# A two-layer hybrid encoder step: the output projection and the residual stream from feature-major to token-major, and retention's padded queries made by another engine

## The chip, the cores and the metric

The kernel runs on 1 core of one Trainium2 chip. The metric is the device time of one execution in microseconds, lower is better. The kernel before takes 2413.29 us, the median of 3 runs (2411.71 to 2414.96). All data are 32-bit floats. Every large product is computed in three passes on numbers split into a high and a low part.

## The reference

Two layers run over 1152 tokens: 1024 of a prompt and 128 of eight running streams (nine chunks of 128 tokens). D_MODEL is 1024, the mixer width 2048. Each layer computes the following, and a root-mean-square norm closes the network:

```python
hn = rmsnorm(x, norm_w)
proj = jnp.einsum("btd,dc->btc", hn, w_in).astype(f32)
# four branches (mLSTM, retention, SSD, HGRN2), each a chunkwise recurrence with its own gate
mix = jnp.concatenate([out_m, out_r, out_s, out_h], axis=-1).astype(x.dtype)
y = x + jnp.einsum("btc,cd->btd", mix, w_out)
# after the last layer
return rmsnorm(x, final_norm_w), stacked
```

Retention, per head and chunk, scores queries against keys and adds what the state gives:

```python
s = jnp.einsum("bhlk,bhsk->bhls", q, k) * dec
o = einsum("bhls,bhsv->bhlv", s, v) + decayed * einsum("bhlk,bhkv->bhlv", q, s_prev)
```

## The kernel before

Weights come in slabs of 256 columns. `slab_load` (L348) fetches one, `slab_split` (L362) splits it into `hi` and `lo` (ScalarE copies the high part, VectorE or GpSimd subtracts), and `slab_run` (L378) multiplies. It has two forms. In "fm" (feature-major, L396 to L413) 128 weight columns are stationary and 384 tokens move: 6 output tiles a slab, each 8 x 3 matmuls of 384 columns (L404 to L406). In "tm" (token-major, L414 to L436) 128 tokens are stationary and the slab's 256 columns move: 9 chunk tiles a slab, each 8 x 3 matmuls of 256 columns (L425 to L427). Both load new weights for every matmul.

Ten units (HGRN2 `h`, retention `r`, SSD `s`, mLSTM `m`) share out the input projection. While TensorE projects one unit, the recurrence (`mix`) of the unit before is woven into the same instruction stream by `merge` (L1775), which counts steps of both. Work that is to come some steps later is put off with `later(lag, ...)` and issued by `tick` (L176), which comes twice in each output tile of either form. Nothing is reordered after that: each engine runs its instructions in this written order, and one that waits holds up all behind it.

The output projection (`out_half`, L1916) runs after the units, in two halves of the mixer width, four slabs each. Half 0 is woven with the last HGRN2 recurrence, half 1 runs alone. Before the change all eight slabs are "fm", and x lives feature-major in DRAM (`xd`). For layer 0's half 0 the input is token-major, so `flip` (L1854) transposes each of the 24 tiles on TensorE and ScalarE copies it back. `ev` (L1919) adds the product to x, and in half 1 sums squares over features with ScalarE and VectorE (`sumsq`, L499).

At the end of half 1 `finish` (L1909) runs for each group of 384 tokens. In layer 0 it sums over partitions with a matmul against ones (`colsum`, L507) and makes the next layer's split input (`norm_group`, L513). In layer 1 `final` (L1960) takes the sums, transposes 24 blocks a group back to token-major, scales and stores them.

In retention's `mix` (L1018) `Z` transposes queries and keys of a chunk and copies them from PSUM on ScalarE; `by_head` (L719) then makes the queries padded per head, on GpSimd; `A` (L1042) scores. In mLSTM's `mix` the first `Z` (L950) is also a `by_head` on GpSimd, written after `use_wi(0)` (L797), whose product needs a row loaded from DRAM. In SSD's `conv` (L1171) the first group of a channel tile clears three columns on GpSimd (L1179).

Of the kernel before, what the change touches and what calls it, by code (L numbers as in the profile page):

```python
# [120 lines left out]
class Kernel:  # L121
    def __init__(self, nc, tc, ctx, T):
# [9 lines left out]
        self.p_t = pool("t", 9)  # L132
# [88 lines left out]
    def setup(self):  # L221
# [3 lines left out]
        self.xd = [self.p_dram.tile([KT, 128, NTOK], F32, name=f"xd{i}") for i in range(2)]  # L225
# [273 lines left out]
    def sumsq(self, acc, x, first):  # L499
        if first:  # L500
            self.act(acc, x, AF.Square)
        else:
            sq = self.f()
            self.act(sq, x, AF.Square)
            self.tt(acc, acc, sq, ALU.add)

    def colsum(self, acc):  # L507

        ps = self.ps("tr")[:, :G3]
        self.nc.tensor.matmul(ps, self.ones, acc, start=True, stop=True)  # L510
        return ps

    def norm_group(self, l, g, pre, ss, spread):  # L513

        nc = self.nc
        r = self.f()
        self.act(r, ss, AF.Ln, scale=1.0 / D, bias=self.eps)
        self.act(r, r, AF.Exp, scale=-0.5)
        hi = self.p_big.tile([128, KT, G3], F32R, tag="big", name=self.nm("hnh"))
        lo = self.p_big.tile([128, KT, G3], F32R, tag="big", name=self.nm("hnl"))  # L520

        def part(k):
            nc.vector.scalar_tensor_tensor(out=pre[k], in0=pre[k], scalar=self.vB[:, 8 * l + k:8 * l + k + 1], in1=r,
                                           op0=ALU.mult, op1=ALU.mult)
            self.copy(hi[:, k], pre[k], "a")
            self.tt(lo[:, k], pre[k], hi[:, k].bitcast(F32), ALU.subtract, "v" if k % 2 else "p")

        for k in range(KT):
            if spread:
                self.later(k // spread, lambda k=k: part(k))  # L530
            else:
                part(k)
        self.hn[0][g], self.hn[1][g] = hi, lo
# [197 lines left out]
    def unit_m(self, l, p):  # L731
# [38 lines left out]
        def mix():  # L770
# [175 lines left out]

            load_e(0)
            load_wi(0)
            use_wi(0)
            Z(0)  # L950
# [31 lines left out]
    def unit_r(self, l, p):  # L982
# [35 lines left out]
        def mix():  # L1018
            S = self.p_st.tile([128, 2, 128], F32, tag="st", name=self.nm("rS"))
            nc.gpsimd.memset(S, 0.0)  # L1020
            qkT, Pt, om, mx, stt, U, qz = {}, {}, {}, {}, {}, {}, {}
# [8 lines left out]
            def Z(c):  # L1030
                j, i = divmod(c, 2)
# [3 lines left out]
                t = self.t(256)  # L1035
                self.copy(t, tr[:, 0:256], "a")
                qkT[c] = t
                if c == 8:
                    U["zq"] = [self.zq(t[:, 0:128], slice(64 * h, 64 * h + 64)) for h in range(2)]
# [9 lines left out]
            def B(c):  # L1049
# [16 lines left out]
                if c < 8:  # L1066
# [3 lines left out]
                    for h in range(2):  # L1070
                        hs = slice(64 * h, 64 * h + 64)
                        new = tr[hs, 128 * h:128 * h + 128]
                        if c == 0:
                            self.copy(S[hs, h], new, "v")
                        else:
                            self.tt(S[hs, h], S[hs, h], new, ALU.add)
                    nc.vector.tensor_scalar(out=S, in0=S, scalar1=g_, scalar2=None, op0=ALU.mult)
                    if c == 7:
                        for h in range(2):
                            self.dma(T["o_p_r"][l, 2 * p + h], S[64 * h:64 * h + 64, h])  # L1080
# [42 lines left out]
            qz[0] = self.by_head(qkT[0][:, 0:128])  # L1123
# [898 lines left out]
```

## Time and profile before

| what | value |
|---|---|
| median of 3 runs | 2413.29 us |
| profiled execution | 2415.16 us |
| its span, first to last instruction | 2413.4 us |
| mean granted TensorE clock | 0.988 |
| TensorE matmul busy | 2333.9 us, 97% |
| VectorE, ScalarE, GpSimd busy | 1390.7, 1076.4, 976.2 us |

The span is the time from the first to the last instruction of the core; 1.8 us of the execution lie outside of it. Stretches are given in microseconds from the span's start. A matmul's duration in the trace overlaps with the next one's, since they are pipelined, so a rate is read from the number of matmuls in a stretch and not from their mean duration. PEclk is the granted clock of TensorE: 1.00 is 2.4 GHz, 0.50 is 1.2 GHz.

### The profile page before, as it was taken

The numbers are of one execution on the slowest core, as the hardware profiler recorded it, in microseconds if no ns is written. First come the engines' busy times: TensorE is split into PE (matmuls) and PEld (weight loads), VectorE is DVE, ScalarE is ACT, GpSimd is POOL, SyncE is SP. The second block draws the span as 40 slices with busy tenths as digits, with TensorE's granted clock in tenths as the row PEclk, the third lists the DMA queues.
The fourth block names the chain that finished last, engine by engine and source line by source line (L and its number), as shares of the span: only waits on it lengthen the run. The fifth ranks groups of instructions, "written<-read, shape, count | busy, mean of one in ns | idle before, by whom it ended". The sixth has DMA issues, their size and how long they took to land.

```text
span 2413.4 us, 49607 instructions
## 1 busy us (share of the span) xinstructions
PE 2333.9 (97%) x18992; PEld 2258.8 (94%) x18992; DVE 1390.7 (58%) x3419; ACT 1076.4 (45%) x2780; POOL 976.2 (40%) x1179
## 2 busy tenths in 40 slices
PE   7999999999999998999989999999999999999998
PEld 7999999999999998899988999999899999888998
DVE  4756753773765376544368376537737654666443
ACT  6344563434455345433243445634344653454332
POOL 2443344353334335423135334432633452345353
PEclk9999999999999999999989999999999999999999
DMA  5111233221123222536411212323111333225552
GB/s 151 37 49 45 81 91 77 65 60 52 50 83 95 61 72 74 158 114 213 133 37 37 61 54 80 90 65 77 49 48 55 98 78 81 50 85 167 159 170 82
DMA packets 273736, 204.06 MB, mean 85 GB/s; under 512 B 57908, under 2 KB 264140, under 8 KB 273500
## 3 DMA queue, kind: packets, MB, share of 16 engines
q1 hardware_dynamic: 273180, 200.81, 29.2%
q8 instruction: 150, 2.46, 0.4%
q14 instruction: 86, 0.70, 0.1%
q0 software_dynamic: 320, 0.09, 0.0%
HBM read 148.53 MB, written 52.29 MB: 83 GB/s over the span
## 4 chain that ended last, share of the span: by engine, by line
PE 83%; DVE 8%; ACT 3%; issue 2%; DMA 1%; POOL 1%; SPq 1%; DVEq 0%; ACTq 0%; POOLq 0%
PE w L425 11%; PE w L404 11%; PE w L427 11%; PE w L426 11%; PE w L406 11%; PE w L405 11%; DVE f L212 3%; ACT f L215 2%; PE w L1310 1%; SPq L218 1%; DVE c L212 1%; PE w L1624 1%; PE w L1663 1%; PE w L1061 1%; PE w L833 1%
## 5 line engine op out<-in xcount | busy, mean ns | idle before, releaser
L425 PE MATMUL w<-hi,hnh 128*128 128x256 f32 (+1 forms) x2592 | 775.8, 299 | 0.0
L427 PE MATMUL w<-hi,hnl 128*128 128x256 f32 (+1 forms) x2592 | 731.9, 282 | 1.6 <-DVE hnl L492 1.6
L426 PE MATMUL w<-lo,hnh 128*128 128x256 f32 (+1 forms) x2592 | 731.7, 282 | 0.1
L425 PEld LDWEIGHTS w<-hi,hnh 128*128 128x128 f32 x2592 | 493.0, 190 | 6.1 <-issue 1.1
L426 PEld LDWEIGHTS w<-lo,hnh 128*128 128x128 f32 x2592 | 493.1, 190 | 3.5 <-issue 0.3
L427 PEld LDWEIGHTS w<-hi,hnl 128*128 128x128 f32 x2592 | 492.5, 190 | 2.2 <-DVE hnl L492 2.0
L215 ACT ACTIVATE f<-f 128x384 f32<-128x384 f32 (+1 forms) x475 | 244.1, 516 | 434.8 <-DVE f L212 275.0
L215 ACT ACTIVATE c<-c 128x512 f32<-128x512 f32 (+3 forms) x398 | 211.3, 534 | 292.4 <-DVE c L546 205.4
L212 POOL TENSOR_TENSOR f<-f,f 128x384 f32<-128x384 f32 (+2 forms) x268 | 226.7, 854 | 283.3 <-ACT f L215 210.3
L404 PE MATMUL w<-hnh,hi 128*128 128x384 f32 x960 | 339.3, 353 | 0.0
L212 POOL TENSOR_TENSOR lo<-raw,hi 128x512 fp32r<-128x512 f32 x148 | 195.0, 1318 | 332.3 <-ACT hi L202 279.2
L406 PE MATMUL w<-hnh,lo 128*128 128x384 f32 x960 | 324.6, 338 | 0.0
L405 PE MATMUL w<-hnl,hi 128*128 128x384 f32 x960 | 324.3, 338 | 0.0
L404 PE MATMUL w<-mxh,hi 128*128 128x384 f32 x768 | 268.7, 350 | 0.0
L406 PE MATMUL w<-mxh,lo 128*128 128x384 f32 x768 | 261.1, 340 | 0.0
L405 PE MATMUL w<-mxl,hi 128*128 128x384 f32 x768 | 260.9, 340 | 0.0
L212 POOL TENSOR_TENSOR c<-c,c 128x512 f32<-128x512 f32 (+2 forms) x120 | 128.9, 1083 | 221.2 <-ACT c L215 175.6
L212 DVE TENSOR_TENSOR lo<-raw,hi 128x512 fp32r<-128x512 f32 x140 | 114.4, 817 | 134.4 <-ACT hi L202 134.2
L404 PEld LDWEIGHTS w<-hnh,hi 128*128 128x128 f32 x960 | 181.6, 189 | 3.0 <-issue 1.8
L405 PEld LDWEIGHTS w<-hnl,hi 128*128 128x128 f32 x960 | 181.8, 189 | 0.8
L406 PEld LDWEIGHTS w<-hnh,lo 128*128 128x128 f32 x960 | 181.0, 189 | 0.0
L212 DVE TENSOR_TENSOR c<-c,w 128x384 f32<-128x384 f32 (+1 forms) x124 | 73.3, 595 | 184.8 <-PE w L406 121.6
(304 smaller groups left out, 3979.3 us busy)
## 6 DMA issues: line engine op xcount, KB each, us to landing
raw<-in_w_in SPq DMA_DIRECT2D x224, 128.0 KB
raw<-in_w_in SPq DMA_DIRECT2D x112, 256.0 KB
c<-mixd SPq DMA_DIRECT2D x96, 192.0 KB
raw<-in_w_out SPq DMA_DIRECT2D x64, 256.0 KB
xd<-c SPq DMA_DIRECT2D x66, 192.0 KB
mixd<-c SPq DMA_DIRECT2D x48, 256.0 KB
c<-xd SPq DMA_DIRECT2D x60, 192.0 KB
c<-sscr SPq DMA_DIRECT2D x36, 256.0 KB
```

Source lines behind the costliest of these rows:

```text
L212: (self.nc.vector if e == "v" else self.nc.gpsimd).tensor_tensor(out=out, in0=a, in1=b, op=op)
L215: self.nc.scalar.activation(out=out, in_=in_, func=func, scale=scale, bias=bias, **k)
L218: (e or self.nc.sync).dma_start(out=out, in_=in_)
L404: nc.tensor.matmul(o, hi[:, k, ms], xhi[:, k, :], start=(k == 0), stop=False)
L405: nc.tensor.matmul(o, hi[:, k, ms], xlo[:, k, :], start=False, stop=False)
L406: nc.tensor.matmul(o, lo[:, k, ms], xhi[:, k, :], start=False, stop=(k == KT - 1))
L425: nc.tensor.matmul(o, xhi[:, k, ts], hi[:, k, :w], start=(k == 0), stop=False)
L426: nc.tensor.matmul(o, xhi[:, k, ts], lo[:, k, :w], start=False, stop=False)
L427: nc.tensor.matmul(o, xlo[:, k, ts], hi[:, k, :w], start=False, stop=(k == KT - 1))
L833: nc.tensor.matmul(sc[:, 0:256], k[g][:, cs], qz.pop(c), start=True, stop=True)
L1061: nc.tensor.matmul(po[h], w[:, h], v[j][:, i, h], start=(c in (0, 8)), stop=(c == 0 or (c < 8 and h == 1)))
L1310: nc.tensor.matmul(po[:, 64 * h:64 * h + 64], pt[:, h], x_[:, 64 * h:64 * h + 64], start=True, stop=True)
```

## The change

All eight slabs of the output projection become "tm": the mixed sequence is stationary, w_out moves. `xd` is kept as nine chunks of 128 tokens x 1024 features, x is fetched two chunks by 256 features at a time, and `flip` goes. `ev` adds on VectorE, ScalarE sums squares of each chunk with its accumulator one tick later, and GpSimd multiplies slabs 0 to 2 with the norm's weight, which now lies along the free axis (`wb`, two rows broadcast from DRAM). `finish` runs for each pair of chunks in the last slab of half 1: two small additions, the inverse root, and the scaling of four pieces. In layer 1 the pieces are stored as they are. In layer 0 `enter` transposes each chunk (8 transposes on TensorE) and splits it out of PSUM into the next layer's input. `sumsq`, `colsum`, `norm_group` and `final` go.

In retention VectorE makes the padded queries from PSUM in `Z`, into a tile of the pool "f" beside the keys; the state is one 128-column tile, and each head's query takes its own product with it (two of 128 columns in place of one of 256). In mLSTM `Z(0)` is written ahead of the loads. In `conv` the clearing goes: the taps of the first group start later instead. The pool "t" has 8 tiles in place of 9.

```diff
-        self.p_t = pool("t", 9)
+        self.p_t = pool("t", 8)
...
-        self.xd = [self.p_dram.tile([KT, 128, NTOK], F32, name=f"xd{i}") for i in range(2)]
+        self.xd = [self.p_dram.tile([NCH, 128, D], F32, name=f"xd{i}") for i in range(2)]
...
+    def enter(self, c, y):
+        g, o = divmod(c * 128, G3)
+        if o == 0:
+            self.hn[0][g] = self.p_big.tile([128, KT, G3], F32R, tag="big", name=self.nm("hnh"))
+            self.hn[1][g] = self.p_big.tile([128, KT, G3], F32R, tag="big", name=self.nm("hnl"))
+        for a in range(2):
+            ps = self.ps("tr")
+            for b in range(4):
+                nc.tensor.transpose(ps[:, 128 * b:128 * b + 128], y[2 * a + b // 2][:, 128 * (b % 2):128 * (b % 2) + 128], self.ident)
+            p3 = ps.rearrange("p (k t) -> p k t", k=4)
+            hi, lo = [x[g][:, 4 * a:4 * a + 4, o:o + 128] for x in self.hn]
+            self.copy(hi, p3, "a")
+            self.tt(lo, p3, hi.bitcast(F32), ALU.subtract)
...
+            Z(0)
             load_e(0)
             load_wi(0)
             use_wi(0)
-            Z(0)
...
-                t = self.t(256)
-                self.copy(t, tr[:, 0:256], "a")
+                t = self.f()
+                self.tt(t[:, 0:256].rearrange("p (h t) -> p h t", h=2), tr[:, None, 0:128].to_broadcast([128, 2, 128]),
+                        self.HM[:, :, None].to_broadcast([128, 2, 128]), ALU.mult)
+                self.copy(t[:, 256:384], tr[:, 128:256], "a")
...
-                nc.tensor.matmul(sc, qkT[c][:, 128:256], qz.pop(c), start=True, stop=True)
+                nc.tensor.matmul(sc, qkT[c][:, 256:384], qkT[c][:, 0:256], start=True, stop=True)
...
-                if 0 < c < 8:
-                    nc.tensor.matmul(pb[:, 0:256], qt[:, 0:128], S.rearrange("p h e -> p (h e)"), start=True, stop=False)
                 for h in range(2):
-                    nc.tensor.matmul(po[h], w[:, h], v[j][:, i, h], start=(c in (0, 8)), stop=(c == 0 or (c < 8 and h == 1)))
+                    if 0 < c < 8:
+                        nc.tensor.matmul(po[h], qt[:, 128 * h:128 * h + 128], S, start=True, stop=False)
+                    nc.tensor.matmul(po[h], w[:, h], v[j][:, i, h], start=(c in (0, 8)), stop=(c < 8))
...
-            qz[0] = self.by_head(qkT[0][:, 0:128])
...
-            if g == 0:
-                nc.gpsimd.memset(t[:, 0:3], 0.0)
-            else:
+            if g > 0:
...
-            def flip(x):
-                ps = self.ps("tr")
-                for cc in range(3):
-                    cs = slice(128 * cc, 128 * cc + 128)
-                    nc.tensor.transpose(ps[:, cs], x[:, cs], self.ident)
-                self.copy(x, ps[:, 0:G3], "a")
...
+            ss = self.p_lay.tile([128, NCH, 4], F32, name="xss")
+            def prefetch(half, s, c, l=l, xin_=xin_):
+                n = 1 if c == 8 else 2
+                x = self.t(256) if half == 1 and n == 1 else self.c(512)[:, :256 * n]
+                x = x.rearrange("p (c d) -> p c d", d=256)
+                cols = slice(256 * s, 256 * s + 256)
+                if l > 0 or half == 1:
+                    self.dma(x, self.xd[(l + half) % 2][c:c + n, :, cols].rearrange("c p d -> p c d"))
+                elif n == 2:
+                    self.dma(x, T["x_prompt"][0, 128 * c:128 * c + 256, cols].rearrange("(c p) d -> p c d", p=128))
                 else:
+                    self.dma(x[:, 0], self.x_rows(c)[:, cols])
+                xin_[s, c] = x
...
+            def finish(c, n, l=l, xfin=xfin, ss=ss):
+                r = self.s(16)
+                self.tt(r[:, 0:2 * n].rearrange("p (c b) -> p c b", b=2), ss[:, c:c + n, 0:2], ss[:, c:c + n, 2:4], ALU.add)
+                self.tt(r[:, 4:4 + n], r[:, 0:2 * n:2], r[:, 1:2 * n:2], ALU.add)
+                self.rstd_small(r[:, 8:8 + n], r[:, 4:4 + n], 1.0 / D)
+                xs = [xfin.pop((s, c)) for s in range(4)]
+                for i in range(n):
+                    rs = r[:, 8 + i:9 + i]
+                    y = [x[:, i] for x in xs]
+                    for s in range(3):
+                        self.copy(y[s], y[s], "ava"[s], scale=rs)
+                    if l + 1 < DEPTH:
+                        y[3] = self.f(256)
+                    nc.vector.scalar_tensor_tensor(out=y[3], in0=xs[3][:, i], scalar=rs, in1=wb[1][:, 256:512], op0=ALU.mult, op1=ALU.mult)
+                    if l + 1 < DEPTH:
+                        self.later(2 + i + (c == 2 and i == 1), lambda i=i, y=y: self.enter(c + i, y))
+                if l + 1 == DEPTH:
+                    for s in range(4):
+                        cols = slice(256 * s, 256 * s + 256)
+                        if c < 8:
+                            self.dma(T["o_yp"][128 * c:128 * c + 256, cols].rearrange("(c p) d -> p c d", p=128), xs[s])
+                        else:
+                            self.dma(T["o_ys"][:, cols], xs[s][:, 0])
...
+                    def ev(c, n, ps):
+                        x = xin_.pop((s, c))
+                        w3 = wb[s // 2][:, None, 256 * (s % 2):256 * (s % 2) + 256].to_broadcast([128, n, 256]) if half else None
+                        p3 = ps[:, :256 * n].rearrange("p (c d) -> p c d", d=256)
+                        self.tt(x, x, p3, ALU.add)
                         if half == 0 or l + 1 < DEPTH:
+                            self.dma(self.xd[(l + 1) % 2][c:c + n, :, 256 * s:256 * s + 256].rearrange("c p d -> p c d"), x)
+                        if half == 0:
+                            return
+                        xfin[s, c] = x
+                        def squares(s=s):
+                            for i in range(n):
+                                self.act(p3[:, i], x[:, i], AF.Square, accum_out=ss[:, c + i, s:s + 1])
+                            if s < 3:
+                                self.later(1, lambda: self.tt(x, x, w3, ALU.mult, "p"))
+                            else:
+                                finish(c, n)
+                        self.later(1, squares)
...
-                    for tk in self.slab_run(si, "fm", mixes[half], ev):
+                    for tk in self.slab_run(si, "tm", mixes[half], ev):
...
+            wb = [self.c(512), self.c(512)]
+            for a in range(2):
+                src = T["norm_w"][l + 1] if l + 1 < DEPTH else T["final_norm_w"]
+                self.dma(wb[a], src[None, 512 * a:512 * a + 512].to_broadcast([128, 512]))
```

GpSimd at the start of an mLSTM unit's recurrence, before: `mC` is the state that is cleared, `f_5079` the row loaded from DRAM times the queries (`use_wi`), `t_5085` the padded queries of chunk 0 (`Z(0)`), `lo` the low part of a slab.

```order
L212 TENSOR_TENSOR lo_4915<-raw_2_4739,hi_4914 128x2x256
L777 MEMSET mC_5075 128x258
L212 TENSOR_TENSOR f_5079<-f_5079,f_4912 128x384
L212 TENSOR_TENSOR t_5085<-f_4912,cst 128x256
L212 TENSOR_TENSOR t_5110<-f_4912,cst 128x256
```

The same place after:

```order
L212 TENSOR_TENSOR lo_4909<-raw_2_4733,hi_4908 128x2x256
L757 MEMSET mC_5069 128x258
L212 TENSOR_TENSOR t_5071<-f_4906,cst 128x256
L212 TENSOR_TENSOR f_5075<-f_5075,f_4906 128x384
L212 TENSOR_TENSOR t_5104<-f_4906,cst 128x256
```

The first padded queries now stand ahead of the product that needs the loaded row.

GpSimd at the start of retention's recurrence (unit r, layer 0), before: `t_2415` and `t_2470` are the padded queries of chunks 0 and 1, `f_2435` the product that closes the first SiLU of `conv`, `rS` the state.

```order
L1020 MEMSET rS_2393 128x256
L212 TENSOR_TENSOR t_2415<-t_2398,cst 128x256
L1179 MEMSET c_2432 128x3
L212 TENSOR_TENSOR lo_2438<-raw_0_2102,hi_2437 128x2x256
L212 TENSOR_TENSOR f_2435<-f_2435,f_2460 128x384
L212 TENSOR_TENSOR t_2470<-t_2420,cst 128x256
L1179 MEMSET c_2489 128x3
```

After, the padded queries are VectorE's: `f_2398` and `f_2419` for chunks 0 and 1, ahead of the first taps (L1176) of `conv`.

```order
L526 TENSOR_SCALAR c_2381<-w_2351 128x256
L212 TENSOR_TENSOR f_2398<-w_2395,cst 128x256
L212 TENSOR_TENSOR f_2419<-w_2416,cst 128x256
L1176 SCALAR_TENSOR_TENSOR f_2434<-c_2432,vA,f_2434 128x381
L1176 SCALAR_TENSOR_TENSOR f_2434<-c_2432,vA,f_2434 128x382
L1176 SCALAR_TENSOR_TENSOR f_2434<-c_2432,vA,f_2434 128x383
L526 TENSOR_SCALAR f_2434<-f_2434 128x384
```

The queries of chunk 1 no longer stand behind the SiLU's product on GpSimd.

TensorE in the last slab of layer 0's half 1, before: L510 is `colsum` of group 0, between two output tiles.

```order
L404 MATMUL w_14413<-mxh_13544,hi_14150 128x384
L405 MATMUL w_14413<-mxl_13545,hi_14150 128x384
L406 MATMUL w_14413<-mxh_13544,lo_14151 128x384
L510 MATMUL w_14450<-f_13710,ones 128x384
L404 MATMUL w_14466<-mxh_13544,hi_14150 128x384
L405 MATMUL w_14466<-mxl_13545,hi_14150 128x384
```

After: L509 are the transposes of chunk 0 (`enter`), one chunk tile behind the pair whose sums they need.

```order
L426 MATMUL w_14697<-lo_14378,mxh_13484 128x256
L427 MATMUL w_14697<-hi_14377,mxl_13485 128x256
L509 MATMUL w_14731<-cst,c_13652 128x128 x2
L509 MATMUL w_14731<-cst,c_13990 128x128 x2
L509 MATMUL w_14738<-cst,c_14263 128x128 x2
L509 MATMUL w_14738<-cst,f_14690 128x128 x2
L425 MATMUL w_14697<-hi_14377,mxh_13621 128x256
```

Three sums over a group become nine pieces of eight transposes, the last two of them within the next layer's first slab.

## Rows read from the trace of the kernel before

**Rows 1.** Stretches, TensorE alone: length, busy (matmuls), granted clock, DMA share, GB/s.

```profile
1109.76:1184.90 75.14, 75.14 (x434) 1.00 0.56 169
385.72:394.24 8.52, 8.52 (x74) 1.00 0.31 79
1233.98:1249.12 15.14, 15.14 (x123) 1.00 0.20 50
```

**Rows 2.** Stretches: the output projection's four parts, TensorE alone.

```profile
968.78:1109.76 140.98, 136.14 (x1120) 0.98 0.52 158
1109.76:1230.96 121.20, 113.83 (x632) 0.94 0.44 131
2167.16:2295.99 128.83, 125.86 (x1049) 0.99 0.54 169
2295.99:2413.40 117.41, 110.38 (x667) 0.99 0.36 122
```

**Rows 3.** Groups by line: layer 0's flips.

```profile
L1859 PE MATMUL w<-cst,c 128*128 128x128 f32 x72 | 12.6, 278 | 4.8 <-DMA c<-in_x_prompt 4.8
```

**Rows 4.** Whom TensorE waited for: us in total, times, longest.

```profile
PE w L1045 <- POOL c L1179: 7.9, 4, 2.0
...
PE w L833 <- POOL t L212: 3.7, 4, 0.9
```

**Rows 5.** Timeline, layer 1's transposes of the second group, 24 in all: start, length, instruction.

```profile
2395.85 0.52 PE L1972 MATMUL w<-cst,c 128*128 128x128 f32 x3
...
2398.39 0.27 PE L1972 MATMUL w<-cst,f 128*128 128x128 f32 x1
2398.42 0.42 PE L404 MATMUL w<-mxh,hi 128*128 128x384 f32 x1
```

**Rows 6.** Groups by line: the kinds of which the new chain is made.

```profile
L212 DVE TENSOR_TENSOR c<-c,w 128x512 f32<-128x512 f32 x40 | 27.3, 684 | 30.2 <-PE w L1336 15.8 <-POOL c L212 8.5 <-PE w L1089 5.9
L215 ACT ACTIVATE c<-c 128x256 f32<-128x256 f32 x148 | 60.8, 416 | 71.8 <-DVE c L822 62.6 <-DVE c L546 6.2
L215 ACT ACTIVATION_READ_ACCUMULATOR t<-w 128x1 f32 x72 | 15.1, 209 | 0.0
L212 DVE TENSOR_TENSOR s<-s 128x2 f32<-128x2 f32 x108 | 21.7, 201 | 28.9 <-ACT s L215 22.4 <-issue 1.3 <-DVE s L212 0.2
L215 ACT ACTIVATE s<-s,eps 128x2 f32<-128x2 f32 x72 | 21.2, 294 | 129.4 <-DVE s L1099 66.8 <-DVE s L212 59.8 <-issue 2.7
```

**Rows 7.** Timeline: the end of the kernel, from the last matmul.

```profile
2402.52 0.33 PE L406 MATMUL w<-mxh,lo 128*128 128x384 f32 x1
2402.89 0.55 DVE L212 TENSOR_TENSOR f<-f,w 128x384 f32<-128x384 f32 x1 [2.94 <-PE w L406]
...
2409.49 0.38 SPq L218 DMA_DIRECT2D out_ys<-c  x1
```

**Rows 8.** Timeline: GpSimd and TensorE at chunk 1 of retention, then chunk 0 of mLSTM.

```profile
200.57 1.00 POOL L212 TENSOR_TENSOR f<-f,f 128x384 f32<-128x384 f32 x1 [3.21 <-ACT f L215]
...
202.19 0.99 PE L1045 MATMUL w<-t,t 128*128 128x256 f32 x2 [1.97 <-POOL c L1179]
...
420.23 1.04 POOL L212 TENSOR_TENSOR f<-f,f 128x384 f32<-128x384 f32 x1 [10.61 <-DVE s L205]
...
421.94 0.70 PE L833 MATMUL w<-t,f 128*128 128x256 f32 x2 [0.93 <-POOL t L212]
```

**Rows 9.** Stretches after waits or among transposes, TensorE alone.

```profile
2383.64:2386.80 3.16, 3.16 (x31) 1.00 0.00 0
1223.00:1229.80 6.80, 4.87 (x18) 0.50 0.08 29
202.50:205.90 3.40, 3.40 (x14) 0.50 0.30 77
1796.50:1799.90 3.40, 3.40 (x15) 0.50 0.29 77
603.20:606.60 3.40, 3.40 (x21) 1.00 0.32 77
```

More of the change, by code (lines that the diff above doesn't have):

```diff
@@ L1018, in mix @@
         def mix():
-            S = self.p_st.tile([128, 2, 128], F32, tag="st", name=self.nm("rS"))
-            nc.gpsimd.memset(S, 0.0)
-            qkT, Pt, om, mx, stt, U, qz = {}, {}, {}, {}, {}, {}, {}
+            S = self.p_st.tile([128, 128], F32, tag="st", name=self.nm("rS"))
+            qkT, Pt, om, mx, stt, U = {}, {}, {}, {}, {}, {}
             gl = self.cst[:, C_GL:C_GL + 4]
@@ L1934, in out_half @@
+                    seq = [(half, s, c) for c in range(0, NCH, 2)]
                     if s < 3:
-                        seq += [(half, 2 * s + 2 + m, 0) for m in range(2)]
+                        seq += [(half, s + 1, c) for c in (0, 2)]
                     elif half == 0:
-                        seq += [(1, m, 0) for m in range(2)]
+                        seq += [(1, 0, c) for c in (0, 2)]
                     n = -1
-                    for tk in self.slab_run(si, "fm", mixes[half], ev):
+                    for tk in self.slab_run(si, "tm", mixes[half], ev):
@@ L1943, in out_half @@
                         n += 1
-                        if n % 2 == 0 and n // 2 + 2 < len(seq):
-                            prefetch(*seq[n // 2 + 2])
-                        if n % 4 == 3 and s == 3:
-                            if half == 0:
-                                load(1, n // 4)
-                            else:
-                                self.later(3, lambda g=n // 4: finish(g))
+                        if n % 4 == 0 and n // 4 + 2 < len(seq):
+                            prefetch(*seq[n // 4 + 2])
@@ L1951, in out_half @@
+                        if n % 6 == 5 and s == 3 and half == 0:
+                            load(1, n // 6)
                         yield True
                     si += 1
-            self.merge(out_half(0), 192, prev["mix"](), prev["steps"])
+            self.merge(out_half(0), KT * NCH * 4, prev["mix"](), prev["steps"])
+            wb = [self.c(512), self.c(512)]
+            for a in range(2):
+                src = T["norm_w"][l + 1] if l + 1 < DEPTH else T["final_norm_w"]
+                self.dma(wb[a], src[None, 512 * a:512 * a + 512].to_broadcast([128, 512]))
@@ L1955, in run @@
             prev = None
-            self.merge(out_half(1), 192)
+            self.merge(out_half(1), KT * NCH * 4)
         while self.queue:
             self.tick()
-    def final(self, g, pre, acc):
-        nc, T = self.nc, self.T
-        tr = self.ps("tr")
-        for cc in range(3):
-            nc.tensor.matmul(tr[:, cc:cc + 1], acc[:, 128 * cc:128 * cc + 128], self.ones[:, 0:1], start=True, stop=True)
-        r = self.s(16)
-        self.rstd_small(r[:, 0:3], tr[:, 0:3], 1.0 / D)
-        for a in range(2):
-            for cc in range(3):
-                c = 3 * g + cc
-                ps = self.ps(("pj", "sc")[a])
-                for b in range(4):
-                    nc.tensor.transpose(ps[:, 128 * b:128 * b + 128], pre[4 * a + b][:, 128 * cc:128 * cc + 128], self.ident)
-                o = self.c(512)
-                if a:
-                    nc.vector.tensor_scalar(out=o, in0=ps, scalar1=r[:, cc:cc + 1], scalar2=None, op0=ALU.mult)
-                else:
-                    self.act(o, ps, AF.Copy, scale=r[:, cc:cc + 1])
-                if c < 8:
-                    self.dma(T["o_yp"][128 * c:128 * c + 128, 512 * a:512 * a + 512], o)
-                else:
-                    self.dma(T["o_ys"][:, 512 * a:512 * a + 512], o)
```

77 lines of the change are left out of this document (11 added, 66 removed).

## The prediction

> **What bounds the kernel now.** The table of the page first: TensorE has matmuls in flight for 97% of the span, and no other engine reaches 60%. So time is lost or won in TensorE's own instruction stream: how many matmuls, at what rate, and how long it stands. The next view is the table by stretches, because matmul durations overlap and only counts over time give a rate. In 75.14 us of undisturbed feature-major work 432 matmuls of 384 columns run (434 shown, two reach in from outside): 0.1739 us each, 4.17 us for a tile of 24. In 8.52 us of undisturbed token-major work 72 of 256 columns run: 0.1183 us each, 2.84 us a tile; with 272 columns it is 120 in 15.14 us, 0.1262 [rows 1]. Per column the narrow ones cost 2% more.
>
> The third view is the four parts of the output projection (layer 0 half 0, half 1 with the first two tiles of layer 1, layer 1 half 0, half 1 to the end). Each has 24 tiles, 100.2 us at the full rate; they take 140.98, 121.20, 128.83 and 117.41 us [rows 2]. What is over the 100.2 is woven-in recurrence in the halves 0, and waits, small matmuls and the tail in the halves 1. The fourth view, the waits, names two places elsewhere that the change touches [rows 4].
>
> **Streaming.** 96 tiles of 24 x 384 columns become 144 of 24 x 256. By rate a part goes from 576 x 0.1739 = 100.2 to 864 x 0.1183 = 102.2 us, so +2.1 in each of four parts, +8.2. Bounds: the same price per column gives 0, the 0.1262 of the 272-column row gives +8.8 a part. I take 0.1183, which is the same instruction with the same shape.
>
> The Trainium skill (TensorE: Matmul & The Clock Gate, "Back-to-back issue gap") gives N/2.4 + 2.5 ns for a warm matmul of N columns. That is 109.2 and 162.5 ns here, and the loss would be 0.7 us a part, 2.9 in all. The trace has 9 and 11 ns more for each, and its rates are used.
>
> **Layer 0, half 0.** The 72 flips of x go, and with them the waits for x_prompt, 4.8 us [rows 3]. 24 transposes start within 2.54 us, one every 0.110 us [rows 5], so the 72 take 7.9. Layer 1's half 0 is the same work with the same recurrence and no flips, and is shorter by 140.98 - 128.83 = 12.2 us [rows 2]. x now arrives token-major and is added by VectorE, off TensorE's path, fetched two pairs of chunks ahead. I take 12.2 (bounds 7.9 and 12.2): with the streaming, **-10.1** here and **+2.1** in layer 1's half 0.
>
> **The boundary between the layers.** Before, the part had 100.2 + two tiles of 3.03 + 15.0 us of sums over partitions, waits and half clock. After, 72 transposes stand in it, 7.9 us at 0.110. Going back from them to the projection costs 0.09 each time (0.26 in place of 0.17 us [rows 5]), 0.8 for nine pieces. Their waits: from the last matmul of a pair of chunks VectorE starts 0.37 us later, as at the end of the kernel [rows 7], and adds (0.68). ScalarE squares two chunks and reads two accumulators (2 x (0.42 + 0.21) = 1.25), VectorE adds twice (0.40), ScalarE takes the root (0.29 and about 0.2) and scales the first piece (0.42) [rows 6]. With some 0.15 for hand-overs that is 3.8 us. The transposes are written one tile, 2.84 us, behind: TensorE waits about 0.9. Four pairs wait so, the fifth has the next layer's first tile as cover; with a slab's split now and then in ScalarE's way I take 4.0. One fall of the clock adds about 1.2. In sum 102.2 + 6.1 + 7.9 + 0.8 + 4.0 + 1.2 = 122.2: **+1.0**. Bounds: no waits and no fall, -4; the whole chain bare at five pairs (18.8) and no less elsewhere, +16.
>
> **Layer 1, half 1 and the end.** Sums, transposes and copies of the first two groups stand in TensorE's stream, 3.16 us for one of them [rows 9], 6.3 for two, and go. At the end it takes 6.97 us from the last matmul to the last store's issue and 3.91 from there to the end of the span, 10.88 together [rows 7]. After, the last chunk's chain is 0.4 (VectorE), but ScalarE is then still at the pair before: its chain of 3.8 and three more copies of 0.42 began 2.84 us earlier, so it is free 2.3 us after the last matmul. Then square 0.63, sums 0.45, root 0.55, two copies 0.83 and one more store's issue 0.38 (as in the last row of [rows 7]) make 5.1; with 3.9 it is 9.1. Sum: 102.2 + 9.1 = 111.3 against 117.41: **-6.1** (bounds -4, with the old tail, and -7.5, with ScalarE free).
>
> **Starts of the recurrences.** In four retention units the queries of chunk 1 wait on GpSimd behind a SiLU product, which waits 3.21 us for ScalarE [rows 8]; TensorE waits 7.9 us in all [rows 4]. After, VectorE makes them, ahead of the taps in its order and some 6 us before they are needed. In four mLSTM units the first padded queries wait behind a product that waits 10.61 us for a loaded row [rows 8]: 3.7 us on TensorE [rows 4]. After, they come first. What is late next in both places is VectorE's work on the scores, for which TensorE has other tiles in between. After two of these waits the clock fell: 14 and 15 matmuls in 3.40 us, where the same place in another unit has 21 [rows 9], a third less, 2.1 us together. Sum **-13.7** (bounds 0, if other waits take their place, and -13.7). The padded queries load VectorE with 36 products of about 0.42; they are made two chunks ahead, and I take nothing. If they made its evictions late, they would take back the 7.9. The state's product is split into two of half the columns, 28 times: nothing, or 2.5 at a re-entry's 0.09 each way. Clearing, smaller taps and the pool of 8 are off TensorE's path.
>
> **The sum.** -10.1 + 1.0 + 2.1 - 6.1 - 13.7 = -26.8 us. It is made against the profiled execution: 2415.16 - 26.8 = 2388.4. The median of the runs lies 1.9 below that execution, so the forecast is 2386.5 us, 1.1% faster.
>
> **Rivals.**
> - *The whole chain is exposed at the boundary.* For it: the same engines split the next slab's weights there, and before, TensorE stood in this part for most of its 15 us. Against it: a tile lies between in the new order. 18.8 in place of 4.0: +14.8, 2401 us.
> - *Other waits take the place of those at the units' starts.* For it: the next instructions on the same path depend on ScalarE, which has work there. Against it: the rows show one cause each. If 3 of the 13.7 remain, 2397 us.
> - *The flips were not what cost layer 0's half 0.* For it: that part has waits in its recurrence too. Then x's new fetch changes nothing but the transposes' place, and the 12.2 stay: 2399 us.
> - *Both of the first two.* -26.8 + 14.8 + 10.7: -1.3, 2412 us, no change.
> - *Slower: the clock falls at the boundary and stays low.* The place is the last slab of layer 0 and the first of layer 1, 25.6 and 27.2 us at full rate, cut by nine pieces of transposes and their waits. At half clock 21 matmuls became 14 or 15 [rows 9], some 45% more time: +24, on top of the bare chain's 14.8: +12, 2425 us. It decides from about 12 us of loss on top of that chain. For it: after the waits at this boundary the clock was at 0.50 for 6.80 us [rows 9]. Against it: a stretch of 24 transposes in 3.16 us kept 1.00 [rows 9]. The Trainium skill (TensorE: Matmul & The Clock Gate, "Part 4: PE-mode transpose") says that transposes do not count as TensorE activity as other matmuls do; by that rule this rival would be likelier, and the row of 3.16 us does not bear it out.
> - *The narrow matmuls cost less than the rows say*, +2.9 in place of +8.2: 2381 us. For it only a faster stream of w_out; against it the measured rate.
>
> **How the numbers follow.** The forecast has 0.54, the exposed chain 0.14, the other waits 0.12, both 0.06, the flips 0.06, the low clock 0.06, the cheaper stream 0.02. A measurement of this kernel can tell about 0.2%, 4.8 us, from no change. Below 2408.5 lie the forecast, the chain, the waits, the flips and the cheaper stream: 0.88 faster; the pair of rivals is 0.06 the same, the clock 0.06 slower. The forecast's own range is 2378 to 2394. The range goes from 2377 (the boundary without waits, the shorter tail) to 2404 (the exposed chain with a little more) and leaves out the pair, the clock and a little below.
>
> **What would show it.** Right: 72 matmuls of 256 columns in 8.5 us in the halves 1; layer 0's half 0 as long as layer 1's, about 131 us; the boundary part near 122 us, with waits of about 1 us before the transposes; the last stretch near 111 us; no waits at the scoring matmuls of retention and mLSTM. Wrong: waits of 3 us and more before the transposes, a granted clock of 0.50 over both slabs, or new waits of TensorE for VectorE in the retention units.

## Result: 1.3% faster, and the profile after

The kernel after takes 2382.44 us, the median of 4 runs (2380.94 to 2387.25), against 2413.44 us before in runs beside it: ratio 0.9875, 95% interval 0.9858 to 0.9892. The forecast was 2386.5. The profiled execution took 2383.27 us with a span of 2381.4, at a mean granted clock of 0.994.

The four parts of the output projection after, in the table by stretches (TensorE alone), to be held against [rows 2]:

```profile
961.54:1091.68 130.14, 127.12 (x1336) 0.99 0.53 164
1091.68:1211.13 119.45, 117.36 (x986) 1.00 0.48 144
2139.21:2270.40 131.19, 127.06 (x1337) 0.99 0.53 164
2270.40:2381.40 111.00, 102.70 (x866) 0.98 0.42 136
```

Half 0 of layer 0 is 10.9 us shorter and now as long as half 0 of layer 1, which is 2.4 us longer. The boundary part is 1.7 us shorter, the last part 6.4. The rest lies outside of these parts: the stretch ahead of the first is 7.2 us shorter (968.78 to 961.54), and layer 1's units between the second and the third 8.1 (936.20 to 928.08). In sum 32.0 us of the span; the two profiled executions differ by 31.9.

The rate of the narrow matmuls within the projection, which [rows 1] could give only from elsewhere, read over one slab, from its first matmul to the next slab's first:

```profile
2296.26:2321.82 25.56, 25.56 (x219) 1.00 0.53 170
```

A slab has 9 tiles of 24, so 216 of the 219 are its own: 0.1183 us each, as had been taken.

TensorE's waits after, where [rows 4] had L1045 and L833:

```profile
PE w L1671 <- DVE f L1662: 12.5, 4, 4.1
...
PE w L509 <- ACT c L202: 1.9, 4, 0.5
```

Neither scoring matmul is in the list any more. L509, the transposes of `enter`, is new, with 1.9 us. The long waits at the top (L1671) belong to HGRN2's recurrence, which the change leaves alone. Before had three of them, 8.3 us; the fourth, 3.0 us in layer 0's half 0, stands where the flips had waited for x_prompt, and the run without flips takes it up.

GpSimd and TensorE at chunk 1 of retention, then at chunk 0 of mLSTM, the places of [rows 8]; L1027 and L813 are the scoring matmuls now:

```profile
198.15 0.59 PE L1027 MATMUL w<-f 128*128 128x256 f32 x2
...
198.64 1.01 POOL L212 TENSOR_TENSOR f<-f,f 128x384 f32<-128x384 f32 x1 [3.21 <-ACT f L215]
...
414.52 1.04 POOL L212 TENSOR_TENSOR f<-f,f 128x384 f32<-128x384 f32 x1 [10.04 <-DVE s L205]
...
415.14 0.60 PE L813 MATMUL w<-t,f 128*128 128x256 f32 x2
```

Both products still wait on GpSimd as long as before, 3.21 and about 10 us. Nothing that TensorE needs stands behind them: the two PE rows have no idle time in brackets.

The boundary, from the last matmul of the first pair of chunks to its transposes (timeline, all engines):

```profile
1174.42 0.28 PE L427 MATMUL w<-hi,mxl 128*128 128x256 f32 x1
...
1174.74 0.69 DVE L212 TENSOR_TENSOR c<-c,w 128x512 f32<-128x512 f32 x1 [5.26 <-PE w L427]
...
1175.46 0.39 ACT L215 ACTIVATE w<-c 128x256 f32<-128x256 f32 x1 [4.71 <-DVE c L212]
1175.79 0.19 ACT L215 ACTIVATION_READ_ACCUMULATOR w<-c 128x1 f32 x1
...
1176.33 0.19 ACT L215 ACTIVATION_READ_ACCUMULATOR w<-c 128x1 f32 x1
1176.55 0.16 DVE L212 TENSOR_TENSOR s<-xss 128x4 f32<-128x4 f32 x1 [1.12 <-ACT w L215]
...
1176.94 0.29 ACT L215 ACTIVATE s<-s,eps 128x2 f32<-128x2 f32 x1 [0.42 <-DVE s L212]
...
1177.50 1.71 ACT L202 ACTIVATE c<-c,s 128x256 f32<-128x256 f32 x4
...
1178.07 0.88 PE L509 MATMUL w<-cst,c 128*128 128x128 f32 x6 [0.53 <-ACT c L202]
```

This is the chain that the prediction built from [rows 6], in its order. From the place of the next matmul (1174.42 + 0.12) to the first transpose it takes 3.5 us, of which the next tile covers 3.0; TensorE stands 0.53.

The end, against [rows 7]:

```profile
2372.82 0.28 PE L427 MATMUL w<-hi,mxl 128*128 128x256 f32 x1
```

```profile
2374.07 0.48 DVE L1899 SCALAR_TENSOR_TENSOR c<-c,s,c 128x256 f32<-128x256 f32 x1
...
2374.47 0.41 DVE L212 TENSOR_TENSOR t<-t,w 128x256 f32<-128x256 f32 x1
...
2376.94 1.83 SPq L218 DMA_DIRECT2D out_ys<-t  x4
```

From the start of the last matmul to the end of the span it is 8.6 us, where it was 10.9. The last addition (L212) starts 1.65 us after that matmul: VectorE is still scaling the pair before (L1899).

### The profile page after: what moved, and what is told of

It is laid out like the page before. It is cut to its first block, busy times and chain, and to the rows that moved or that the text cites. A ratio compares the mean times of both kernels' runs of the same rounds, so it can differ in the third digit from the quotient of the medians.

```text
span 2381.4 us, 51682 instructions
## 1 busy us (share of the span) xinstructions
PE 2315.6 (97%) x20104; PEld 2251.8 (95%) x20104; DVE 1367.5 (57%) x3426; ACT 1082.4 (45%) x2881; POOL 935.8 (39%) x1117
## 4 chain that ended last, share of the span: by engine, by line
PE 84%; DVE 8%; ACT 4%; DMA 1%; issue 1%; SPq 1%; POOL 1%; ACTq 0%; DVEq 0%; POOLq 0%
PE w L425 16%; PE w L427 16%; PE w L426 16%; PE w L404 6%; PE w L405 6%; PE w L406 6%; DVE f L212 3%; ACT f L215 2%; PE w L1289 1%; DVE c L212 1%; DMA c<-mixd 1%; PE w L1642 1%; PE w L1603 1%; PE w L1552 1%; PE w L1043 1%
## 5 line engine op out<-in xcount | busy, mean ns | idle before, releaser
L215 ACT ACTIVATE f<-f 128x384 f32<-128x384 f32 (+1 forms) x460 | 236.3, 516 | 427.7 <-DVE f L212 263.5
L212 POOL TENSOR_TENSOR f<-f,f 128x384 f32<-128x384 f32 (+2 forms) x268 | 225.6, 849 | 290.7 <-ACT f L215 216.3
L425 PE MATMUL w<-hi,mxh 128*128 128x256 f32 x1152 | 329.4, 286 | 0.0
L427 PE MATMUL w<-hi,mxl 128*128 128x256 f32 x1152 | 325.2, 282 | 0.2 <-POOL mxl L212 0.2
L426 PE MATMUL w<-lo,mxh 128*128 128x256 f32 x1152 | 324.9, 282 | 0.0
L212 POOL TENSOR_TENSOR lo<-raw,hi 128x512 fp32r<-128x512 f32 x148 | 196.4, 1327 | 304.3 <-ACT hi L202 278.3
L212 POOL TENSOR_TENSOR c<-c,c 128x512 f32<-128x512 f32 (+2 forms) x144 | 160.3, 1122 | 273.3 <-ACT c L215 169.5
L425 PEld LDWEIGHTS w<-hi,mxh 128*128 128x128 f32 x1152 | 219.0, 190 | 1.4 <-issue 0.6
L427 PEld LDWEIGHTS w<-hi,mxl 128*128 128x128 f32 x1152 | 219.0, 190 | 0.8 <-POOL mxl L212 0.8
L426 PEld LDWEIGHTS w<-lo,mxh 128*128 128x128 f32 x1152 | 218.2, 189 | 0.0
L212 DVE TENSOR_TENSOR lo<-raw,hi 128x512 fp32r<-128x512 f32 x140 | 114.8, 820 | 149.9 <-ACT hi L202 149.7
```

The source lines that it names most:

```text
L212: (self.nc.vector if e == "v" else self.nc.gpsimd).tensor_tensor(out=out, in0=a, in1=b, op=op)
L215: self.nc.scalar.activation(out=out, in_=in_, func=func, scale=scale, bias=bias, **k)
L425: nc.tensor.matmul(o, xhi[:, k, ts], hi[:, k, :w], start=(k == 0), stop=False)
L426: nc.tensor.matmul(o, xhi[:, k, ts], lo[:, k, :w], start=False, stop=False)
L427: nc.tensor.matmul(o, xlo[:, k, ts], hi[:, k, :w], start=False, stop=(k == KT - 1))
```

## The experiments

The theory after the result: three gains that are independent of each other (the starts of the recurrences, the flips, the sums and transposes of the end), against a dearer stream; at the boundary the chain behind each pair is almost covered by one tile. The main rival for the starts: other waits would have come in their place, and the projection alone gave the time.

**One part alone, then the other.** The first kernel is before with the retention, mLSTM, conv and pool edits alone; the second is after with just those undone.

```diff
+            Z(0)
             load_e(0)
             load_wi(0)
             use_wi(0)
-            Z(0)
...
-                nc.tensor.matmul(sc, qkT[c][:, 128:256], qz.pop(c), start=True, stop=True)
+                nc.tensor.matmul(sc, qkT[c][:, 256:384], qkT[c][:, 0:256], start=True, stop=True)
...
```

> The kernel before with only the edits at the starts of the recurrences (retention's queries made by VectorE, the smaller state, mLSTM's first queries written first, no clearing, pool t of 8); the output projection stays feature-major. Theory (these edits take away one wait at each of four retention and four mLSTM starts, and nothing else): 4 x 2.2 + 4 x 1.1 us and two falls of the clock of 1.5 us, -16 us, 2397 us, and the four parts of the output projection as long as before. Rival (part of what the changed kernel gained at these places comes from the new output projection, through tiles and queues): -10 us or less, 2403 us or more.

> The changed kernel with those same edits undone: only the output projection, residual stream and norm are token-major. Theory (the two halves of the change add up): -10.9 in layer 0's half 0, -1.7 at the boundary, +2.4 and -6.4 in layer 1, -16 us with a little spread from falls of the clock, 2397 us. Rival (the halves are not independent: VectorE and GpSimd are loaded otherwise in each): the two gains of this run and of the one before miss the 31 us of both together by 6 us or more.

The first took 2399.58 us (2394.91 to 2400.81), ratio 0.9937, interval 0.9915 to 0.9958: about -15 us. The second took 2400.52 (2398.34 to 2402.98), ratio 0.9942, interval 0.9924 to 0.9961: about -14. The ratios multiply to 0.9879, against 0.9875 for both together: the two halves of the change add and do not hide each other, to within the intervals (some 5 us each way). The parts of the projection in each, by stretches, first the starts alone:

```profile
957.88:1098.45 140.57, 135.98 (x1121) 0.98 0.52 158
1098.45:1219.95 121.50, 112.91 (x632) 0.96 0.43 132
2148.44:2275.55 127.11, 124.37 (x1048) 1.00 0.55 171
2275.55:2392.90 117.35, 110.38 (x667) 0.99 0.36 121
```

then the projection alone:

```profile
967.26:1099.45 132.19, 128.10 (x1337) 0.97 0.53 165
1099.45:1218.42 118.97, 117.06 (x987) 1.00 0.48 143
2157.86:2290.59 132.73, 128.18 (x1337) 0.97 0.52 164
2290.59:2401.20 110.61, 102.40 (x866) 0.97 0.42 134
```

With the starts alone the four parts stay those of [rows 2]; with the projection alone they are those of after, to within 2 us, which is as much as a fall of the clock more or less makes (PEclk 0.97 against 0.99). Outside of them the starts alone shortened four slabs of retention by 3.8, 2.2, 2.2 and 3.7 us and four of mLSTM by 1.2 each, 16.7 in all, counted from each slab's first matmul to the next slab's. The other 64 of the 72 slabs kept their lengths within 0.1 us, but for seven of -1.8 to +1.6, where falls of the clock or waits for x came out otherwise. So no wait of such a size came in their place. In the second kernel's list of waits the scoring matmuls are back, word for word those of [rows 4] but for the lines:

```profile
PE w L1026 <- POOL c L1160: 7.9, 4, 2.0
...
PE w L813 <- POOL t L212: 3.7, 4, 0.9
```

**The flips alone.** Before, with layer 0's transposes of x left out, so that another residual is added there:

```diff
-                    self.later(FLIP, lambda: flip(x))
```

> The kernel before with the flips of layer 0 left out (x_prompt is loaded by the same transfers, but its 24 tiles are added untransposed, so the residual of layer 0 is other numbers). Theory (the flips cost TensorE their transposes and the waits for x_prompt, which stand in its order only through them): layer 0's half 0 falls from 141.0 to 129 to 130 us. Rival 1 (only the 72 transposes counted, 7.9 us): 133 us. Rival 2 (the part is long for its recurrence's waits): 139 us or more.

```profile
967.63:1096.49 128.86, 125.96 (x1048) 0.99 0.56 168
```

That part falls from 140.98 to 128.86 us: 12.1, where 12.2 had been taken from the comparison with layer 1. One run, 2403.73 us. The rival that the part is long for its recurrence's waits falls. But the 12.1 are not all the flips' own. Before, the clock stood at 0.50 for 6.8 us of this part, here for 3.4. The run without the clearing (below) has the flips and also 3.4 us at 0.50; against it the difference is 9.2, with 3.4 us of waits for x_prompt in place of 4.8:

```profile
970.09:1108.11 138.02, 134.66 (x1120) 0.99 0.53 161
```

And the flips' waits had covered another one. Without them the transposes of HGRN2's recurrence wait in this part, which before they did not:

```profile
PE w L1692 <- DVE f L1683: 2.9, 1, 2.9
```

**The cover at the boundary, half a tile less.** After, with the transposes one tick earlier:

```diff
-                        self.later(2 + i + (c == 2 and i == 1), lambda i=i, y=y: self.enter(c + i, y))
+                        self.later(1 + i + (c == 2 and i == 1), lambda i=i, y=y: self.enter(c + i, y))
```

> The changed kernel with the transposes at the layer boundary put off by 1 tick and not 2 after a pair's sums, so half a chunk tile, 1.42 us, closer. Theory (the chain from a pair's last matmul to its first transposes takes about 3.3 us, since TensorE waited 0.5 us at 2.84): waits of about 1.9 us before four first transposes, about 6 us more in the boundary part, 125 us in place of 119.5, the granted clock at 1.00. Rival 1 (the waits were ScalarE's queue and not the chain's length): waits stay at about 0.5 us, 120 us. Rival 2 (waits and transposes at this spacing drop the clock for both slabs): 0.50 over 20 us and more, 140 us or more.

It took 2391.86 us in one run. Its waits before the transposes, from the list, and the boundary part:

```profile
PE w L509 <- ACT c L202: 9.5, 4, 3.7
...
PE w L509 <- ACT t L202: 2.4, 1, 2.4
```

```profile
1090.18:1219.37 129.19, 117.26 (x986) 1.00 0.44 131
```

The part is 9.7 us longer than after's, and the waits 11.9 in place of 1.9: the whole of it. Three of the four waits are 1.94 or 1.95 us, which is 0.53 plus the 1.42 of half a tile, as expected. The part was expected near 125 us and came out at 129, for two reasons. The last chunk waits too (2.4 us), and one wait is 3.70. For that one VectorE's timeline shows the cause, in this kernel:

```profile
1192.44 1.29 DVE L212 TENSOR_TENSOR hnl<-w,hnh 128x512 fp32r<-128x512 f32 x2 [3.31 <-ACT hnh L202]
...
1193.64 0.68 DVE L212 TENSOR_TENSOR c<-c,w 128x512 f32<-128x512 f32 x1
...
1197.01 0.88 PE L509 MATMUL w<-cst,c 128*128 128x128 f32 x6 [3.70 <-ACT c L202]
```

and at the same place in after:

```profile
1190.21 0.69 DVE L212 TENSOR_TENSOR c<-c,w 128x512 f32<-128x512 f32 x1 [0.52 <-PE w L427]
1191.28 1.29 DVE L212 TENSOR_TENSOR hnl<-w,hnh 128x512 fp32r<-128x512 f32 x2 [0.38 <-ACT hnh L202]
```

`hnl` is the split of the chunk that was transposed just before, the other row the addition that starts the next pair's chain. In after the addition stands first; half a tile earlier the split does, and the addition waits behind it. The pair's last matmul starts at 1191.61 here, so the addition comes 2.0 us after it where the row of after's first pair has 0.32: the 1.7 us between them, on top of 1.95, make the 3.70. So the place decides an order on VectorE as well, which the expectation had not looked at. The clock stayed at 1.00 over the whole part, through a wait of 3.70 us: nothing in this run speaks for the rival that the clock falls at the boundary.

**What stood ahead of retention's queries.** The list of waits [rows 4] names the clearing of three columns (L1179) as the releaser; the prediction named the SiLU product ahead of it. Before, without the clearing alone:

```diff
-            if g == 0:
-                nc.gpsimd.memset(t[:, 0:3], 0.0)
-            else:
+            if g > 0:
...
```

> The kernel before with one edit alone: SSD's conv no longer clears three columns on GpSimd (its first taps start later instead). Padded queries stay on GpSimd. My theory: at chunk 1 of retention the row names the clearing as the last releaser, but the queries behind it still stand behind the SiLU's product, which waits 3.21 us for ScalarE; TensorE's four waits at the scoring of retention stay at 6 to 8 us in all and the time within 2 us of before. Rival: the clearing that the trace names is what held TensorE; then the 7.9 us of waits go to below 2 and the kernel is 8 to 10 us shorter.

```profile
PE w L1045 <- POOL t L212: 7.9, 4, 2.0
```

The waits are the same 7.9 us in four; now the list names the queries' own instruction. GpSimd at chunk 1 there, on its timeline:

```profile
199.04 0.99 POOL L212 TENSOR_TENSOR f<-f,f 128x384 f32<-128x384 f32 x1 [3.21 <-ACT f L215]
199.99 1.63 POOL L212 TENSOR_TENSOR t<-t,cst 128x256 f32<-128x256 f32 x2
```

The product waits its 3.21 us for ScalarE and the queries follow at its end. One run gave 2415.97 us, beside one of before with 2420.43. Since before's other runs reach from 2407.84 to 2419.67, these 4 us are within its own scatter and say nothing; the waits decide, and they have not moved. So the clearing cost TensorE nothing here.

**mLSTM's order alone.** Before, with `Z(0)` written first.

> The kernel before with one edit alone: in mLSTM the padded queries of chunk 0 are written ahead of the product that needs the loaded row. Theory: the waits at the scoring of mLSTM, 3.7 us in four, go, and the four stretches with them get 0.9 to 1.2 us shorter each, 4 to 5 us in all; retention's 7.9 us stay. Rival (other waits take their place): TensorE stands as long at the next instruction of the recurrence that needs ScalarE or VectorE, and the time stays within 1 us.

One run, 2410.37 us. L833 is gone from the list of waits and L1045 still stands there with 7.9 us. The four slabs with these waits, from first matmul to the next slab's first, got 1.2 us shorter each, 4.7 in all, and the same in after to 0.05 us. The first of them, in before and here:

```profile
419.32:458.37 39.05, 38.12 (x295) 1.00 0.27 75
```

```profile
416.04:453.92 37.88, 37.88 (x294) 1.00 0.27 78
```

The waits listed are 0.93 us each: what a wait cost here is about 0.25 us more than the list shows.

**The cover, half a tile more.** After, with the transposes one tick later.

```diff
-                        self.later(2 + i + (c == 2 and i == 1), lambda i=i, y=y: self.enter(c + i, y))
+                        self.later(3 + i, lambda i=i, y=y: self.enter(c + i, y))
```

> The kernel after with the transposes of the next layer's input one tick (half a tile, about 1.4 us) later, at 3 + i for every pair. Theory: the chain behind a pair ends at most 0.5 us after the transposes' place now, so the four waits of 0.5 us before the transposes go and the boundary part (119.45 us) becomes about 117.5; the last pair, which moves 1.4 us later against the next layer's first group, costs nothing since that group's tiles do not need it yet. Rival: the last chunk's split comes later and the next layer's tile of its group waits for it, or a wait appears at the first tile of the third group: 119 to 122.

```profile
1092.32:1209.23 116.91, 116.65 (x986) 1.00 0.49 148
```

The part is 2.5 us shorter, with busy 116.65 of 116.91, and L509 is no longer in the list of waits. One run gave 2382.39 us, the time of after: in both halves 0 the clock stood at 0.50 for 6.8 us where it was 3.4 in after, and they are 2.2 and 1.2 us longer (132.36 and 132.40).

**Fewer, wider matmuls.** After, with two matmuls of 256 columns joined into one of 512 in the output projection; the sums over the two are left out.

```diff
...
+                            if k % 2 == 0:
+                                wide = ps[:, 0:512].rearrange("p (a b) -> p a b", a=2)
+                                h2, l2 = hi[:, k:k + 2, :256], lo[:, k:k + 2, :256]
+                                nc.tensor.matmul(wide, xhi[:, k, ts], h2, start=(k == 0), stop=False)
...
```

> The kernel after with the output projection's matmuls joined in pairs: 512 moving columns (the 256 of two inner tiles) in one instruction, half as many instructions, the same number of columns streamed; the sums of the two inner tiles land in different columns, so the output leaves out adding them. It asks whether the 8.2 us of dearer streaming are a fixed cost per instruction. Theory: the two rates (0.1739 us for 384 columns, 0.1183 for 256) lie on a line of 0.434 ns a column and 7 ns an instruction; 512 columns then take 0.229 us, 432 of them 99.1 us a part in place of 102.2, 3.1 us a part and 12.5 in all (by 0.4167 ns a column and 11 ns an instruction 0.2243, 96.9, 21 in all). So 2361 to 2370 us. Rival: the cost goes with the columns (0.462 ns each at this width, whoever moves them): no change, 2381.

```profile
2270.00:2360.00 90.00, 90.00 (x387) 1.00 0.37 118
```

386 in 90 us are 0.233 us each, where two narrow ones take 0.237: about 1.5 us a part for half the instructions. The four parts were 1.3, 1.8, 0.6 and 1.7 us shorter, 5.5 together (in the third the clock stood at 0.50 for 6.8 us, in after's for 3.4), and the one run took 2378.17 us. That is less than half of the expected 12.5 and not nothing: a price per instruction of some 3 to 4 ns, not 7 to 11. Both expectations failed. What is left of the difference between the forms (0.453 ns a column at 384 feature-major, 0.456 at 512 and 0.462 at 256 token-major) stays open, since no run has 512 columns in the feature-major form.

**A version with both small gains.** After, with the transposes one tick later and the last chunk written to two tiles and stored by two DMAs, and beside it after itself again.

```diff
...
+                if wide:
+                    for a in range(2):
+                        self.dma(T["o_ys"][:, 512 * a:512 * a + 512], yo[a])
...
```

> The kernel after with two edits: the transposes one tick later (as in the run before it), and the last chunk's four scaled pieces written into two tiles and stored by two DMAs in place of four. Theory: the boundary part is 2 to 2.5 us shorter than after's 119.45 (it was 116.91 with the first edit alone); at the end the four issues of the last stores take 1.83 us on SP, two take 0.9, and the last stretch is about 0.9 us shorter than after's 111.0; in sum 3 us, 0.12%, below the kernel after run beside it. Rival: the last store's landing sets the end whatever the number of issues (larger transfers land later), and falls of the clock elsewhere even out the boundary: no difference from after.

> The kernel after once more, unchanged, timed beside the run before it on the same chip: the ratio to before should again be 0.986 to 0.989, with 0.9875 the value measured first.

It took 2380.31 us (2377.88 to 2383.85), ratio 0.9862, interval 0.9847 to 0.9877; after beside it took 2383.29 (2383.02 to 2384.93), ratio 0.9873, interval 0.9857 to 0.9889. The median is 3.0 us lower; the intervals overlap, so it is not shown to be faster than after. The boundary and the last part:

```profile
1089.38:1205.54 116.16, 116.16 (x987) 1.00 0.49 146
2266.21:2377.10 110.89, 102.71 (x866) 0.99 0.43 135
```

```profile
2372.87 0.84 SPq L218 DMA_DIRECT2D out_ys<-c  x2
```

The first edit did what the run before had shown. The second did nothing: the issues take 0.84 us in place of 1.83, and the last part is as long as after's (110.89 and 111.00). From the start of these issues to the end of the span it is 4.2 us here and 4.5 in after, so their number is not what sets the end. From the start of the last of them it is 3.8 and 3.0 us, which fits the expectation's rival that larger transfers land later; no run tests it, and what sets the end is open.

## Why the prediction was right

The mechanism was right in its main steps, and the sum (-26.8) was 5 us short of the profiled difference of 31.9. In its own steps:

- **Streaming, +2.1 a part.** Held: 0.1183 us in the projection itself, and layer 1's half 0, where only the form changes, is 2.4 us longer. The Trainium skill (TensorE: Matmul & The Clock Gate, "Back-to-back issue gap") gives N/2.4 + 2.5 ns as the gap of an isolated matmul at full clock, and says that in a stream with a weight load for each matmul both set the spacing. An estimate by its formula is 109.2 ns for these 256 columns; this trace has 118.3, and the trace decides. Its fixed part of 2.5 ns is not far from the 3 to 4 ns that the wide matmuls showed; the price per column is where the two differ.
- **Layer 0, half 0, -10.1.** Measured -10.9, in part by luck; so the term of the flips was right in kind and its size unsure. In the 12.2 taken for the flips, as in the 12.1 of the run without them, is a difference of the clock: 6.8 us at 0.50 before, 3.4 in both parts that it was held against. At like clock the flips were 9.2, in a run with 1.4 us less of waits for x_prompt. Their waits for x_prompt were not all gained, since one of HGRN2's stands there now. After's own half 0 took 128.04 us in one run with no fall, 130.14 in this one with 3.4 us at 0.50, and 132.36 in one with 6.8.
- **The boundary, +1.0.** Measured -1.7: the mis-sized term. Two of its pieces were too dear. The waits were 1.9 us and not 4.0: the chain is 3.5 us, not 3.8, since ScalarE's accumulator reads overlap the squares (1.06 us for two in place of 1.25), and TensorE was busy for 3.0 of it, not 2.84. A wait of 0.5 us is the small difference of two terms of 3.5 and 3.0, so an error of 0.4 in them, here from durations that overlap, nearly doubles it. And the fall of the clock that was put in as likely (1.2) did not come: 1.00 over the part in after, in the run with longer waits and in the later ones.
- **Layer 1, half 1 and the end, -6.1.** Measured -6.4. The end from the last matmul's start takes 8.6 us and not 9.1. Which engine is late was not as told: VectorE's part was put at 0.4 us after the last matmul and ScalarE named as the one still at work, but VectorE's scaling of the pair before holds the addition until 1.65 us after, and ScalarE is free (2374.78) just before that addition ends (2374.88). The two delays are nearly equal, which is luck.
- **Starts of the recurrences, -13.7.** Measured by the slabs' starts -16.6: retention 3.8, 2.2, 2.2 and 3.7, mLSTM 4.7. It was mis-sized in two places. A wait of 1.97 us cost 2.2 and one of 0.93 cost 1.2, so the list shows about 0.25 us less than a wait costs; that it counts from the modelled ends of matmuls in flight would explain it, but was not tried. And each fall of the clock behind such a wait cost 1.5 us, not 1.05. Two slabs of retention in before, the first with a fall, and the second in after:

```profile
189.53:224.55 35.02, 33.05 (x187) 0.95 0.14 37
590.53:624.01 33.48, 31.52 (x187) 1.00 0.15 40
```

```profile
585.21:616.46 31.25, 31.25 (x188) 1.00 0.16 42
```

Of the rivals, the exposed chain needs waits of 3 us and more, and even half a tile earlier only one was that long. What was said for it, that TensorE stood for most of the part's 15 us before, was a misreading: the list of waits has 7.4 there, and the rest is small matmuls and low clock. Other waits at the starts did not come: the starts alone gave 15 us, in the eight slabs where they were expected. The flips' rival fell with the run without flips. The low clock at the boundary has no row in its favour, and the stream was no cheaper than its rate.

Part of the profiled 31.9 is chance: falls of the clock at the start and in HGRN2's recurrences stand at other places in every run. Against before, after has one fewer at the kernel's start (1.9 us), two more ahead of layer 0's projection (1.6 each) and one fewer in its half 0 (about 2).

## What to carry to other kernels

A change of many parts can be forecast to a few us when each term is read from one stage and the terms lie in different stages; here the two halves, run alone, added to the whole. Ask of each releaser in a list of waits what stands ahead of it on its engine: the clearing named here cost nothing, and by the timeline it was the product in front of it that held the queries. Before a term is taken from the difference of two stretches, compare the clock in them: a fall more or less was about 2 us of the 12 here. A chain that was to be covered by one tile was better written half a tile later than it seemed to need: half a tile earlier cost 10 us at five places, half a tile later gave 2.5 back.

## What the runs showed of the hardware

Waits of up to 3.70 us of TensorE at the boundary, before its transposes, left the granted clock at 1.00 in the run with the transposes one tick earlier. At the same boundary in before, two waits of 7.4 us in all were followed by it at 0.50 [rows 9], and so were waits of 0.6 to 3.2 us between the small matmuls of HGRN2. One of these in after:

```profile
2069.47 0.56 PE L1564 MATMUL w<-f 128*64 128x64 f32 x6 [3.22 <-POOL f L212]
```

```profile
2070.00:2073.40 3.40, 3.40 (x16) 0.50 0.02 5
```

The same wait of 1.97 us in retention was followed by a fall at two of its four places in before, and at two without the clearing, one of them another (602.8 in place of 202.5): which of them fall changes from kernel to kernel, and each costs about 1.5 us.

A fall is not always paid for. One slab of HGRN2's recurrence in layer 1 had 10.2 us at 0.50 in before and 3.4 in after, and took 45.5 us in both (2087.12 to 2132.63 at a mean granted clock of 0.89, and 2058.83 to 2104.28 at 0.96).

Joining 256 columns to 512 halved the matmuls and took about 1.4% off their time: 0.233 us in place of 2 x 0.1183.
